# Splitting the third gate/up product's activation sum by token half and moving the small sums around it

## The chip, the cores and the metric

The kernel runs on one core of one Trainium2 chip. The metric is the device time of one execution in microseconds (us), the median of several runs. All engines of the core run their own queues: TensorE (PE) for matmuls, with its weight loads beside it, VectorE (DVE), ScalarE (ACT), GpSimd (POOL), and SyncE (SP), which only issues DMAs here.

## The reference

One encoder layer on 256 prompt tokens and 1024 sample tokens (1280 in all, in fp32), then a final norm. What matters here is the hand-over from the output projection to the SwiGLU feed-forward network:

```python
x = x + mix @ w_o
h2 = rmsnorm(x, ffn_norm_g)
x = x + (jax.nn.silu(h2 @ w_gate) * (h2 @ w_up)) @ w_down
```

`h2` has 1024 columns, `w_gate` and `w_up` are 1024 by 2816.

## The kernel before

**Arithmetic.** Every fp32 operand of a large matmul is split into a high part (a rounding cast, on ACT) and a low part (operand minus high part, on DVE or POOL). One logical product is three matmuls (lines 110 to 112, `mm3`): weight high by moving high, weight high by moving low, weight low by moving high. `h2 @ w_gate` and `h2 @ w_up` are done as block products with seven instead of eight products (a Strassen form): the 1280 tokens are two halves T of 640, the 1024 inner columns two halves K, and the weight is blocks 11, 12, 21, 22. `SEQ` gives the products' order: 1, 2, 6, 7, 4, 5, 3. Each needs one sum of weight blocks and one sum of activation blocks.

**Stages around the change.** In the output projection (loop over ten 128-token tiles t, `NT` = 10) `ffn_in(t, x)` makes each tile of `h2`, transposed, into R["11"] (in the trace zA), R["12"] (zA), R["21"] (zB), R["22"] (zB). For the second half of the tokens (t = 5 to 9) it also makes the activation sums in place: R11 = R12 - R11, then T2[t-5] = R22 - R11, which is product 6's activation sum, then (`differences`) R12 = R22 - R12 and R21 = R21 - T2. For t up to 8 these run on POOL (line 888), for the last tile on DVE. T2[0], T2[1] and T2[4] lie in the buffers named A21, A22 and A12, T2[2] and T2[3] in the two buffers named `sum`.

**Splitting an activation sum.** `split_S` (lines 902 and 903) casts on ACT and subtracts on DVE into the pair S[m], high and low, all 640 columns in one tile each. `build_S(6, ())` does it for the first four 128-column parts of product 6, `split_after` for the fifth; the other products' sums are split in two halves of 320 columns.

**Weights.** `split_A` (lines 909 and 910) casts a weight block on ACT and subtracts on POOL into two of six `wc` buffers. `operand(A, m)` makes the sum first (`sum_A`, line 920, on POOL) where the product has one: for 6, s1 = A21 + A22 into a `sum` buffer, s2 = s1 - A11, the split of s2, and s4 = A12 - s2 for product 3; for 7, A21 = A11 - A21.

**The first round (fp = 0).** Its weight blocks for gate (i = 0) and up (i = 1) are loaded by SP into places `at[0]` to `at[7]` inside the two tiles S5, which are free until product 5. The products are issued as gate 1, gate 2, up 1, up 2, then 6, 7, 4, 5, 3 for gate and up in turn; each has two halves s of 320 tokens with 12 matmuls each. The two halves of a product run in two PSUM banks, products 1 and 2 share them, so product 2 may start only when ACT has copied out product 1 (line 990). Up's copies are held behind the cast of gate's operand 6 (`hold`). In the trace S<-A, S<-sum at lines 902 and 903 are product 6's parts, wc<-S at lines 909 and 910 are splits of weights that lie in the S5 tiles, z<-M at line 990 are product 1's and 2's copies.

**What sets the order.** A planner lays out each engine's queue when the kernel is built, by its own estimate of times, with earlier program text first where several instructions are ready; every engine then runs its queue in order. `tc.issue_after(ins)` queues what is traced in it behind `ins` on the engine of `ins`, and nothing more. SP's queue is in program order. A new tile waits for the users of the earlier tiles on its own bytes; a buffer of a ring waits for the readers of its earlier content.

Of the kernel before, what the change touches and what calls it, by code (L numbers as in the profile page):

```python
# [11 lines left out]
F32 = mybir.dt.float32  # L12
F32R = mybir.dt.float32r
# [26 lines left out]
def encoder_trunk(ctx: ExitStack, tc: tile.TileContext, x_tm, x_T, g_attn, w_c, w_v, w_qk,  # L40
# [46 lines left out]
    def rstd_of(out, ss, n):  # L87
        w = out.shape[1]
        nc.gpsimd.tensor_scalar(out=out, in0=ss, scalar1=1.0 / n, scalar2=EPS,
                                op0=ALU.mult, op1=ALU.add)  # L90
        nc.gpsimd.tensor_tensor(out=out, in0=out, in1=mhalf[:, 0:w], op=ALU.pow)
# [709 lines left out]
    mixed = [None]  # L801
# [48 lines left out]
    def ffn_in(t, x):  # L850
# [3 lines left out]
        nc.scalar.activation(h2, x, AF.Square, accum_out=ss)  # L854
        store(xm_d[t], x)
        rstd_of(r, ss, D)
# [26 lines left out]
        difference(eng, T2[t - 5], R["22"][:, :, cs], R["11"][:, :, cs])  # L883
# [22 lines left out]
    def split_A(raw):  # L906
        hi = rY.tile([P, 4, P], F32R, name="wc", bufs=6)
        lo = rY.tile([P, 4, P], F32R, name="wc", bufs=6)
# [13 lines left out]
    def operand(A, m, s2=None, s4=None):  # L922
        if m == 6:
# [5 lines left out]
            if s4:  # L929
                A["s4"] = rY.tile([P, 4, P], F32, name=s4)  # L930
            else:
                A["s4"] = A["s2"]
            sum_A(A["s4"], A["12"], A["s2"])
# [41 lines left out]
    l4 = [pool("l4a"), pool("l4z"), pool("l4b")]  # L975
    def product(C, w, m, s, held, bank=None, hold=None):
# [5 lines left out]
        for kc in range(4):  # L982
            mm3(ps, w[0][:, kc], w[1][:, kc], S[m][0][:, kc, cs], S[m][1][:, kc, cs],
                kc == 0 and m not in CHAIN, kc == 3, m in CHAIN)
# [38 lines left out]
    def build_S(m, after):  # L1023
        pl, nm = {6: (l4[0], "S6"), 3: (rA, "zA")}.get(m, (l4[2], f"S{m}"))
        S[m] = [pl.tile([P, 4, NQ], F32R, name=nm, bufs=2) for x in "hl"]
        cuts = [(slice(n * P, (n + 1) * P), T2[n]) for n in range(5)] if m == 6 else [
            (slice(s * NS, (s + 1) * NS), None) for s in range(2)]
        for cs, from_ in cuts[:-1] if m == 6 else cuts:
            after = split_after(m, cs, from_, after)
        return after  # L1030

    def split_after(m, cs, from_, after):
        with ExitStack() as es:
            for ins in after:
                es.enter_context(tc.issue_after(ins))
            return split_S(m, cs, from_)
# [26 lines left out]
    s6 = build_S(6, ())  # L1063
    with tc.issue_after(s6[1]):
        cs8 = slice(3 * P, 4 * P)
        difference(nc.vector, R["21"][:, :, cs8], R["21"][:, :, cs8], T2[3])
    for fp in range(NF // 2):
# [3 lines left out]
        if fp == 0:  # L1071
            spare = [l4[2].tile([P, 4, NQ], F32R, name="S5", bufs=2).bitcast(F32)
                     .rearrange("p a b -> p (a b)").rearrange("p (n a b) -> p n a b", n=5, b=P)
                     for _ in range(2)]
            at = [spare[n // 5][:, n % 5] for n in range(8)]
# [18 lines left out]
            with tc.issue_after(w6[0][3]):  # L1094
                w6.append(operand(A0[1], 6, at[7], "A22"))
# [302 lines left out]
```

## Time and profile before

| what | us |
|---|---|
| three runs | 1618.12, 1614.91, 1615.25 |
| median | 1615.25 |
| profiled execution, own time | 1615.65 |
| profiled execution, first to last instruction | 1613.9 |
| PE busy (share of the span) | 1580.4 (98%) |
| POOL busy | 668.8 (41%) |
| DVE busy | 890.7 (55%) |
| ACT busy | 716.0 (44%) |

The gate/up stage lies between 794.5 and about 1346 us of the span; its first round ends near 848.6 us. A share of busy time is a mean over all stages, so what a change in one place is worth is read from the waits and the order of instructions in that place.

### The profile page before, as it was taken

To read this page: it belongs to the slowest core of one execution; us is meant where nothing else is said; L and a number is where in the kernel's file an instruction comes from. 1 tells how busy PE (TensorE), PEld (TensorE's weight loads), DVE (VectorE), ACT (ScalarE), POOL (GpSimd) and SP (SyncE) were. 2 spreads that over 40 slices of the span, in tenths; PEclk is the share of its full clock that TensorE was granted. 3 is DMA by queue.
4 is the path that set the end of the run, shared out by engine and by line. 5 is a ranking of instruction groups with operands and counts; after the bars stand their busy time and mean duration, and the time that the engine had idled before them with its cause. 6 is when DMAs were issued, how large, how long until landed. Compare 5 with 4: busy or idle time off the path is not lost.

```text
span 1613.9 us, 25762 instructions
## 1 busy us (share of the span) xinstructions
PE 1580.4 (98%) x9616; PEld 1442.6 (89%) x9616; DVE 890.7 (55%) x1483; ACT 716.0 (44%) x1484; POOL 668.8 (41%) x839
## 2 busy tenths in 40 slices
PE   8999999999999999999999999999999999999998
PEld 8987899988888888888899999999999998888886
DVE  5743055556677677443493444334444246886676
ACT  6523154555677777544353223232222332443334
POOL 4631444543211119224676665565666651010002
PEclk9999999999999999999999999999999999999999
DMA  8626212152101030234312232222232237843534
GB/s 292 195 78 159 49 26 61 37 201 67 32 16 30 23 119 11 89 118 144 119 63 72 91 110 97 68 90 89 97 110 76 69 128 265 300 139 96 156 103 156
DMA packets 123247, 171.12 MB, mean 106 GB/s; under 512 B 35505, under 2 KB 67505, under 8 KB 123121
## 3 DMA queue, kind: packets, MB, share of 16 engines
q1 hardware_dynamic: 78880, 120.30, 24.3%
q10 hardware_dynamic: 43680, 46.87, 8.4%
q0 software_dynamic: 560, 2.29, 0.3%
q8 instruction: 76, 1.25, 0.3%
q14 instruction: 51, 0.41, 0.1%
HBM read 118.96 MB, written 50.46 MB: 105 GB/s over the span
## 4 chain that ended last, share of the span: by engine, by line
PE 88%; ACT 3%; DVE 3%; POOL 2%; DMA 1%; issue 1%; SPq 0%; ACTq 0%; POOLq 0%; DVEq 0%
PE M L110 10%; PE M L112 10%; PE M L111 10%; PE d L110 5%; PE d L111 5%; PE d L112 5%; PE o L728 4%; PE tp L718 3%; PE na_o L499 2%; PE po L110 2%; PE po L111 2%; PE po L112 2%; PE pj L110 2%; PE pj L112 2%; PE pj L111 2%; PE S L110 2%
## 5 line engine op out<-in xcount | busy, mean ns | idle before, releaser
L110 PE MATMUL M<-S,wc 128*128 128x320 f32 x1056 | 321.9, 309 | 2.8 <-ACT wc L909 1.5
L111 PE MATMUL M<-S,wc 128*128 128x320 f32 x1056 | 324.2, 308 | 0.0
L112 PE MATMUL M<-S,wc 128*128 128x320 f32 x1056 | 312.3, 309 | 0.9 <-POOL wc L910 0.9
L110 PEld LDWEIGHTS M<-S,wc 128*128 128x128 f32 x1056 | 198.0, 188 | 4.0 <-ACT wc L909 2.0
L111 PEld LDWEIGHTS M<-S,wc 128*128 128x128 f32 x1056 | 198.7, 188 | 0.0
L112 PEld LDWEIGHTS M<-S,wc 128*128 128x128 f32 x1056 | 195.2, 188 | 1.2 <-POOL wc L910 1.2
L910 POOL TENSOR_TENSOR wc<-A,wc 128x512 fp32r<-128x512 f32 x86 | 120.7, 1405 | 79.4 <-ACT wc L909 79.3
L992 DVE TENSOR_TENSOR z<-M,z 128x320 f32<-128x320 f32 x120 | 56.4, 487 | 124.0 <-PE M L112 103.5
L910 POOL TENSOR_TENSOR wc<-sum,wc 128x512 fp32r<-128x512 f32 x62 | 88.5, 1427 | 87.0 <-ACT wc L909 86.9
L909 ACT CAST wc<-A 128x512 fp32r<-128x512 f32 x86 | 53.4, 621 | 157.2 <-PE M L111 137.1
L992 DVE TENSOR_TENSOR zB<-M,zB 128x320 f32<-128x320 f32 x100 | 47.6, 488 | 133.4 <-PE M L112 120.1
L111 PE MATMUL d<-S,S 128*128 128x512 f32 (+1 forms) x314 | 121.2, 386 | 0.0
L112 PE MATMUL d<-S,S 128*128 128x512 f32 (+1 forms) x314 | 120.7, 387 | 0.0
L110 PE MATMUL d<-S,S 128*128 128x512 f32 (+1 forms) x314 | 120.5, 387 | 0.0
L100 DVE TENSOR_TENSOR PT<-tp,PT 128x512 fp32r<-128x512 f32 (+1 forms) x144 | 93.0, 658 | 38.9 <-ACT PT L99 37.7
L909 ACT CAST wc<-sum 128x512 fp32r<-128x512 f32 x62 | 38.3, 618 | 145.0 <-PE M L111 93.4
L99 ACT CAST PT<-tp 128x512 fp32r<-128x512 f32 (+1 forms) x144 | 79.4, 566 | 38.2 <-PE tp L718 34.6
L710 DVE TENSOR_REDUCE mm<-S 128x1 f32<-128x1024 f32 (+1 forms) x80 | 84.8, 1062 | 10.9 <-PE S L112 9.4
L1039 ACT CAST S<-as 128x640 fp32r<-128x640 f32 x58 | 42.2, 728 | 105.5 <-issue 60.2
L741 POOL TENSOR_TENSOR ob<-ob 128x128 f32<-128x128 f32 x40 | 18.4, 461 | 157.2 <-ACT ob L738 149.2
L712 ACT ACTIVATE ex<-S,mm 128x1024 f32<-128x1024 f32 (+1 forms) x80 | 79.7, 996 | 8.0 <-DVE mm L710 7.4
L728 PE MATMUL o<-PT,v 128*128 128x256 f32 x544 | 80.6, 287 | 1.0 <-ACT PT L99 1.0
(429 smaller groups left out, 4120.8 us busy)
## 6 DMA issues: line engine op xcount, KB each, us to landing
as<-act_d SPq DMA_DIRECT2D x73, 320.0 KB
w<-in_w_down_dram SPq DMA_DIRECT2D x44, 256.0 KB
act_d<-z ACTq DMA_DIRECT2D x35, 320.0 KB
act_d<-zB ACTq DMA_DIRECT2D x35, 320.0 KB
A<-in_w_gate_dram SPq DMA_DIRECT2D x42, 256.0 KB
A<-in_w_up_dram SPq DMA_DIRECT2D x42, 256.0 KB
x<-in_x_tm_dram SPq DMA_DIRECT2D x20, 512.0 KB
cT_d<-stg ACTq DMA_DIRECT2D x20, 320.0 KB
```

The source lines that it names most:

```text
L99: i = nc.scalar.copy(out=hi, in_=ps)
L100: nc.vector.tensor_sub(out=lo, in0=ps, in1=hi)
L110: nc.tensor.matmul(out, lhsT=sh, rhs=mh, start=first, stop=False, **kw)
L111: nc.tensor.matmul(out, lhsT=sh, rhs=ml, start=False, stop=False, **kw)
L112: return nc.tensor.matmul(out, lhsT=sl, rhs=mh, start=False, stop=last, **kw).ins
L710: nc.vector.reduce_max(out=nm[:, u:u + 1], in_=S, axis=AX.X, negate=True)
L712: nc.scalar.activation(ex, S, AF.Exp, bias=nm[:, u:u + 1], scale=1.0, accum_out=l[:, u:u + 1])
L718: nc.tensor.transpose(tp[:, j], ex[:, kt * P:(kt + 1) * P], ident)
L728: nc.tensor.matmul(oT, lhsT=vv, rhs=pt[s][g][:, j], start=kt == 0 and s == 0, stop=kt == nkt - 1 and s == 1)
L909: i0 = nc.scalar.copy(out=hi, in_=raw)
L910: i1 = nc.gpsimd.tensor_tensor(out=lo, in0=raw, in1=hi, op=ALU.subtract)
L992: nc.vector.tensor_add(out=o, in0=ps, in1=a)
```

## The change

- **Product 6's activation sum** is kept in four tiles: high and low, for each token half s. `part6(n)` splits 128-column part n into them; part 2 lies across the two halves and is split in two pieces. Part 2 is split first, parts 0 and 1 are queued on ACT behind the last tile's squaring (`last_sq`, line 854), part 3 and part 4 come inside the fp = 0 loop. `product` picks the half's tile for m = 6.
- **T2[3]** (t = 8) is not made in `ffn_in` but on POOL behind the low part of gate's operand 6; part 3 and R21 - T2[3] follow it.
- **Up's operand 2** is split before the loop, its low part on DVE instead of POOL, into places inside the second S5 tile instead of `wc` buffers.
- **Later sums on POOL**: operand 7 is queued behind the low part of up's operand 6; the two s4 (`sum_4`, for product 3) behind the low part of up's operand 7. Before, all of them could be queued as soon as they were ready.
- **Places**: the pool l4b, which held S5, S7 and S4, becomes three: l4b (S5), l4c (one tile S4), l4d (the other S4, and S7). `at[0]` to `at[4]` stay in the first S5 tile, `at[5]` and `at[7]` are in the S4 tile of l4d, `at[6]` in that of l4c, so S4 is written only when s4 of gate and of up have read them.
- `build_S(7)` is queued behind the cast of up's operand 6 on ACT alone. `rstd_of` returns its instruction, `last_rs` isn't used.

```diff
-        nc.scalar.activation(h2, x, AF.Square, accum_out=ss)
+        last_sq[0] = nc.scalar.activation(h2, x, AF.Square, accum_out=ss).ins
...
-        difference(eng, T2[t - 5], R["22"][:, :, cs], R["11"][:, :, cs])
+        if t != NT - 2:
+            difference(eng, T2[t - 5], R["22"][:, :, cs], R["11"][:, :, cs])
...
+    def sum_4(A, nm=None):
+        A["s4"] = rY.tile([P, 4, P], F32, name=nm) if nm else A["s2"]
+        sum_A(A["s4"], A["12"], A["s2"])
...
-            sum_A(A["s4"], A["12"], A["s2"])
+            if s2 is None:
+                sum_4(A)
...
-    l4 = [pool("l4a"), pool("l4z"), pool("l4b")]
+    l4 = [pool("l4a"), pool("l4z"), pool("l4b"), pool("l4c"), pool("l4d")]
...
+            sh, sl = [x[s][:, kc] if m == 6 else x[:, kc, cs] for x in S[m]]
+            mm3(ps, w[0][:, kc], w[1][:, kc], sh, sl, kc == 0 and m not in CHAIN, kc == 3, m in CHAIN)
...
+    def part6(n, after=()):
+        with ExitStack() as es:
+            for ins in after:
+                es.enter_context(tc.issue_after(ins))
+            for s in range(2):
+                a, b = max(n * P, s * NS), min((n + 1) * P, (s + 1) * NS)
+                if a < b:
+                    src = T2[n][:, :, a - n * P:b - n * P]
+                    hi, lo = [x[s][:, :, a - s * NS:b - s * NS] for x in S[6]]
+                    i0 = nc.scalar.copy(out=hi, in_=src).ins
+                    i1 = nc.vector.tensor_sub(out=lo, in0=src, in1=hi).ins
+        return i0, i1
...
-    s6 = build_S(6, ())
-    with tc.issue_after(s6[1]):
-        cs8 = slice(3 * P, 4 * P)
-        difference(nc.vector, R["21"][:, :, cs8], R["21"][:, :, cs8], T2[3])
+    at = blocks(l4[2], "S5", F32)
+    w0[2, 1] = hi, lo = blocks(l4[2], "S5", F32R)[0:2]
+    nc.scalar.copy(out=hi, in_=A0[1]["12"])
+    nc.vector.tensor_sub(out=lo, in0=A0[1]["12"], in1=hi)
+    b, c = blocks(l4[4], "S4", F32, 1), blocks(l4[3], "S4", F32, 1)
+    at += [b[0], c[0], b[1]]
+    S[6] = [[l4[0].tile([P, 4, NS], F32R, name="S6", bufs=4) for _ in range(2)] for _ in range(2)]
+    cs8 = slice(3 * P, 4 * P)
+    part6(2)
+    for n in range(2):
+        part6(n, (last_sq[0],))
...
-                    w0[2, 1] = operand(A0[1], 2)
                     A0[1]["12"] = load_A(1, 0, "12", at[5])
-                    w6 = [operand(A0[0], 6, at[6], "A21")]
+                    w6 = [operand(A0[0], 6, at[6])]
                     hold = w6[0][2]
-                    s6 = split_after(6, slice(4 * P, 5 * P), T2[4], (hold, s6[1]))
+                    with tc.issue_after(w6[0][3]):
+                        difference(nc.gpsimd, T2[3], R["22"][:, :, cs8], R["11"][:, :, cs8])
+                    s6 = part6(3)
+                    with tc.issue_after(s6[1]):
+                        difference(nc.vector, R["21"][:, :, cs8], R["21"][:, :, cs8], T2[3])
+                    s6 = part6(4, s6)
...
-                w = w6 if m == 6 else [operand(A0[i], m) for i in range(2)]
+                with ExitStack() as es:
+                    if m == 7:
+                        es.enter_context(tc.issue_after(w6[1][3]))
+                    w = w6 if m == 6 else [operand(A0[i], m) for i in range(2)]
+                if m == 7:
+                    with tc.issue_after(w[1][3]):
+                        for i in range(2):
+                            sum_4(A0[i], ("A21", "A22")[i])
                 if m != 3:
-                    build_S(SEQ[n + 3], w[1][2:])
+                    build_S(SEQ[n + 3], w[1][2:3] if m == 6 else w[1][2:])
```

## Rows read from the trace of the kernel before

**Rows 1.** The page's busy times: us (share of the span) and number of instructions of an engine.

```profile
PE 1580.4 (98%) x9616; PEld 1442.6 (89%) x9616; DVE 890.7 (55%) x1483; ACT 716.0 (44%) x1484; POOL 668.8 (41%) x839
```

**Rows 2.** The waits of PE over the whole span, those of the gate/up products: who waited for whom, us in total, times, longest us.

```profile
PE M L110 <- ACT wc L909: 1.5, 2, 0.9
PE M L110 <- ACT S L902: 1.2, 1, 1.2
...
PE M L112 <- POOL wc L910: 0.9, 1, 0.9
```

**Rows 3.** PE in order of time, 805 to 815 us and at 853 us: start, us, what, and in brackets the idle time before it with what ended it.

```profile
805.61 0.46 PE L112 MATMUL M<-S,wc 128*128 128x320 f32 x2
806.95 0.41 PE L110 MATMUL M<-S,wc 128*128 128x320 f32 x1 [0.89 <-ACT wc L909]
...
808.75 0.96 PE L110 MATMUL M<-S,wc 128*128 128x320 f32 x2 [1.24 <-ACT S L902]
809.50 0.47 PE L111 MATMUL M<-S,wc 128*128 128x320 f32 x1
...
811.63 0.33 PE L110 MATMUL M<-S,wc 128*128 128x320 f32 x1
...
813.56 0.31 PE L111 MATMUL M<-S,wc 128*128 128x320 f32 x1
...
813.86 0.31 PE L111 MATMUL M<-S,wc 128*128 128x320 f32 x1
...
814.15 0.31 PE L110 MATMUL M<-S,wc 128*128 128x320 f32 x1
...
853.80 0.42 PE L112 MATMUL M<-S,wc 128*128 128x320 f32 x1 [0.93 <-POOL wc L910]
```

**Rows 4.** Busy time by stretch: the first row counts only instructions that write or read the products' PSUM tile M (columns: stretch, length, then PE, PEld, DVE, ACT busy with counts, granted PE clock as a share of full speed, DMA share, GB/s), the others all instructions (with a column for POOL after ACT's).

```profile
794.47:806.07 11.60, 10.96 (x72) 10.46 (x71) 0.00 (x0) 1.45 (x4) 1.00 0.56 183
...
794.47:806.07 11.60, 11.59 (x81) 11.32 (x79) 10.39 (x9) 6.73 (x19) 10.96 (x9) 1.00 0.56 183
806.07:813.86 7.79, 5.67 (x28) 5.38 (x29) 6.91 (x6) 3.66 (x8) 7.71 (x5) 0.78 0.13 34
...
809.00:810.00 1.00, 1.00 (x4) 0.96 (x5) 1.00 (x2) 0.35 (x2) 1.00 (x2) 0.50 0.00 0
...
848.60:860.00 11.40, 10.47 (x72) 10.21 (x71) 6.11 (x6) 3.65 (x8) 8.17 (x6) 1.00 0.38 132
```

**Rows 5.** ACT in order of time, 795 to 809 us.

```profile
795.22 0.64 ACT L902 CAST S<-A 128x512 fp32r<-128x512 f32 x1
...
796.77 1.08 ACT L854 ACTIVATE m<-x 128x1024 f32<-128x1024 f32 x1
...
805.95 0.43 ACT L990 COPY z<-M 128x320 f32<-128x320 f32 x1 [0.89 <-PE M L112]
806.28 0.62 ACT L909 CAST wc<-S 128x512 fp32r<-128x512 f32 x1
808.08 0.62 ACT L902 CAST S<-A 128x512 fp32r<-128x512 f32 x1 [1.18 <-DVE A L888]
808.60 0.75 ACT L990 COPY z<-M 128x320 f32<-128x320 f32 x2
```

**Rows 6.** POOL in order of time, 795 to 825 us, and one instruction of the second round.

```profile
795.91 1.84 POOL L888 TENSOR_TENSOR sum<-zB,zA 128x512 f32<-128x512 f32 x1
...
799.37 1.30 POOL L910 TENSOR_TENSOR wc<-A,wc 128x512 fp32r<-128x512 f32 x1
800.63 1.75 POOL L920 TENSOR_TENSOR sum<-S 128x512 f32<-128x512 f32 x1
802.46 1.65 POOL L920 TENSOR_TENSOR S<-sum,A 128x512 f32<-128x512 f32 x1
804.05 1.76 POOL L920 TENSOR_TENSOR S<-A,S 128x512 f32<-128x512 f32 x1
...
807.46 1.72 POOL L910 TENSOR_TENSOR wc<-S,wc 128x512 fp32r<-128x512 f32 x1
...
815.96 8.82 POOL L910 TENSOR_TENSOR wc<-S,wc 128x512 fp32r<-128x512 f32 x4
...
860.27 1.30 POOL L910 TENSOR_TENSOR wc<-A,wc 128x512 fp32r<-128x512 f32 x1 [3.43 <-ACT wc L909]
```

**Rows 7.** DVE in order of time, 798 to 824 us.

```profile
798.22 0.68 DVE L903 TENSOR_TENSOR S<-sum,S 128x512 fp32r<-128x512 f32 x1
...
801.14 1.79 DVE L903 TENSOR_TENSOR S<-sum,S 128x512 fp32r<-128x512 f32 x1
802.85 1.79 DVE L888 TENSOR_TENSOR zB<-zB,sum 128x512 f32<-128x512 f32 x1
804.57 0.68 DVE L869 TENSOR_TENSOR zA<-trh,gf 128x512 f32<-128x512 f32 x1
...
816.07 2.54 DVE L903 TENSOR_TENSOR S<-zA,S 128x1280 fp32r<-128x1280 f32 x1
...
821.45 2.18 DVE L903 TENSOR_TENSOR S<-zB,S 128x1280 fp32r<-128x1280 f32 x1
```

**Rows 8.** SP's DMA queue in order of time, the last of the six weight loads into the S5 tiles and what follows it.

```profile
795.62 1.19 SPq L64 DMA_DIRECT2D S<-in_w_up_dram  x1
805.84 35.56 SPq L64 DMA_DIRECT2D A<-in_w_gate_dram  x4
```

More of the change, by code (lines that the diff above doesn't have):

```diff
@@ L90, in rstd_of @@
                                 op0=ALU.mult, op1=ALU.add)
-        nc.gpsimd.tensor_tensor(out=out, in0=out, in1=mhalf[:, 0:w], op=ALU.pow)
+        return nc.gpsimd.tensor_tensor(out=out, in0=out, in1=mhalf[:, 0:w], op=ALU.pow).ins
     def split_w(hi, lo, raw):
@@ L799, in load_wo @@
             wo.append(wt)
-    mixed = [None]
+    mixed, last_sq, last_rs = [None], [None], [None]
     def mix_in(t):
@@ L906, in split_A @@
     def split_A(raw):
-        hi = rY.tile([P, 4, P], F32R, name="wc", bufs=6)
-        lo = rY.tile([P, 4, P], F32R, name="wc", bufs=6)
+        hi, lo = [rY.tile([P, 4, P], F32R, name="wc", bufs=6) for _ in range(2)]
         i0 = nc.scalar.copy(out=hi, in_=raw)
@@ L920, in sum_A, with operand @@
         nc.gpsimd.tensor_tensor(out=out, in0=a, in1=b, op=op)
-    def operand(A, m, s2=None, s4=None):
+    def sum_4(A, nm=None):
+        A["s4"] = rY.tile([P, 4, P], F32, name=nm) if nm else A["s2"]
+        sum_A(A["s4"], A["12"], A["s2"])
+    def operand(A, m, s2=None):
         if m == 6:
@@ L928, in operand @@
             w = split_A(A["s2"])
[L929 to L932, printed above, removed]
-            sum_A(A["s4"], A["12"], A["s2"])
+            if s2 is None:
+                sum_4(A)
             return w
@@ L1023, in build_S, with split_after @@
     def build_S(m, after):
[L1024 to L1029, printed above, removed]
+        pl = {3: [rA] * 2, 5: [l4[2]] * 2, 7: [l4[4]] * 2, 4: l4[3:5]}[m]
+        S[m] = [x.tile([P, 4, NQ], F32R, name="zA" if m == 3 else f"S{m}", bufs=1 if m == 4 else 2)
+                for x in pl]
+        for s in range(2):
+            after = split_after(m, slice(s * NS, (s + 1) * NS), after)
         return after
-    def split_after(m, cs, from_, after):
+    def split_after(m, cs, after):
         with ExitStack() as es:
@@ L1035, in split_after @@
                 es.enter_context(tc.issue_after(ins))
-            return split_S(m, cs, from_)
+            return split_S(m, cs)
+    def part6(n, after=()):
+        with ExitStack() as es:
+            for ins in after:
+                es.enter_context(tc.issue_after(ins))
+            for s in range(2):
+                a, b = max(n * P, s * NS), min((n + 1) * P, (s + 1) * NS)
[5 more added lines that the diff above has]
+        return i0, i1
     def split_f(o, raw):
@@ L1061, in down_first, with blocks @@
             ops[5, f] = a_ring[f], w_ring[f]
-    s6 = build_S(6, ())
-    with tc.issue_after(s6[1]):
-        cs8 = slice(3 * P, 4 * P)
-        difference(nc.vector, R["21"][:, :, cs8], R["21"][:, :, cs8], T2[3])
+    def blocks(pl, nm, dt, bufs=2):
+        x = pl.tile([P, 4, NQ], F32R, name=nm, bufs=bufs)
+        x = (x.bitcast(F32) if dt is F32 else x).rearrange("p a b -> p (a b)")
+        x = x.rearrange("p (n a b) -> p n a b", n=5, b=P)
+        return [x[:, n] for n in range(5)]
+    at = blocks(l4[2], "S5", F32)
[9 more added lines that the diff above has]
+        part6(n, (last_sq[0],))
     for fp in range(NF // 2):
@@ L1071, in encoder_trunk @@
         if fp == 0:
[L1072 to L1075, printed above, removed]
             for n, (b, i) in enumerate((("21", 0), ("22", 0), ("21", 1), ("22", 1), ("12", 0),
```

6 lines of the change are left out of this document (2 added, 4 removed).

## The prediction

> **What bounds the kernel now.** I read the page's busy times first: PE is busy for 98% of the span [rows 1], so only the few places where PE stands idle can give anything, unless matmuls are saved, and the change saves none. The waits of PE show what belongs to the gate/up products: three causes, 3.3 us in all [rows 2]; two of the entries have their longest wait in the stretch below. PE in order of time then shows the place that the change touches [rows 3]. From 794.47 to 806.07 us 72 matmuls of 320 columns ran [rows 4], three products of 24: gate 1, up 1, gate 2. The next two waits are 0.89 us for a cast of ACT and 1.24 us for another [rows 3]. ACT's rows name them: wc<-S, the cast of gate's operand 6 (806.28 to 806.90), and S<-A, the last part of product 6's activation sum (808.08 to 808.70) [rows 5]. So the planner had put three matmuls of product 6 ahead of up's product 2, and PE, which runs its queue in order, waited for both. Up 2 could not have filled the place either: the copies of up 1, held behind the first cast, stand behind the second too, at 808.60 [rows 5]. After this idle time the granted clock was 0.50 of full speed, the level of 1.2 GHz [rows 4], and matmuls were (811.63 - 809.50) / 8 = 0.266 us apart instead of (814.15 - 813.56) / 4 = 0.147 [rows 3].
>
> **What the place costs.** From 806.07 to 813.86 PE did the 24 matmuls of up 2 and three of product 6: 27 x 0.147 = 3.97 us of work in 7.79. The loss is 3.82 us: 2.13 idle, about 12 x 0.119 = 1.4 from the clock, the rest between. This is the most that the change can win here. The other wait, 0.93 us at 853.80 [rows 3], lies in the second round, after loads that wait for PE's progress in the first; I leave it where it is, with 0.9 either way in the range. It also shows that an idle time of 0.93 alone left the clock at 1.00 [rows 4].
>
> **The change, part by part.** *Squaring earlier.* ACT cast three parts of product 6 from 795.22 on before the squaring at 796.77 [rows 5]. Parts 0 and 1 now follow it; up's operand 2 and part 2's two pieces may still precede it. Bounds: 0 to 1.4 us earlier; I take 0.7, the middle, since what may still precede it is about half of the three casts. *Operand 2's low part* leaves POOL: 1.30 us [rows 6], and costs DVE one subtract, 0.68 alone to 1.79 beside POOL [rows 7], at a time when DVE only waits for the last tile's scale. With both, POOL starts s1 of gate's operand 6 at 800.63 - 1.3 - 0.7 = 798.6. *T2[3]* leaves POOL's queue ahead of that scale: 1.84 us [rows 6] that ended before the squaring did, so nothing there, and comes back later (below). *Part 2 in two pieces* adds one cast and one subtract; both run before the scale is ready: nothing if so, 0.4 + 0.7 us on ACT and DVE if not. *Four tiles* let product 6's first half start without parts 3 and 4. *Loads*: SP's order is unchanged. The last load's new place covers bytes of the old stage's small gain vector, which DVE's scaling of the last tile reads until 804.57 + 0.68 = 805.25 [rows 7]; SP's next issue came at 805.84 [rows 8], so only this load waits, from 795.62, and its reader, s4 of up, comes after 820. Nothing, and none of the following loads moves.
>
> So gate's operand 6: s1, s2, cast, low part. A POOL instruction of this size took 1.30 us alone and 1.65 to 1.76 beside DVE [rows 6]; I take 1.6, as POOL is sometimes alone in the new order. s2 ends at 798.6 + 3.2 = 801.8, the cast (0.62 + 0.1 for the hand-over) at 802.5, the low part at 804.1. The cast thus falls ahead of ACT's copy at 805.95, up 1's copies follow, and up 2 can start at 806.07. The place closes; product 6 of gate starts at 806.07 + 24 x 0.147 = 809.6 instead of 813.7.
>
> **What is late next.** Now PE wants everything 3.8 us earlier, and POOL, which was busy for 7.71 of the 7.79 us [rows 4], gets two new holds and one chain. The chain: T2[3] on POOL 804.1 to 805.7; ACT's cast 806.4; part 3's low part 0.7 (POOL waits, so DVE is alone) 807.2; R21 - T2[3] 0.7, 807.9. Only then is the second `sum` buffer free for s1 of up's operand 6: 809.5, s2 811.1, cast 811.8, low part 813.4. PE needs this at up 6's third matmul: 809.6 + 24 x 0.147 + 0.3 = 813.4. Just in time. Queued behind it, by the new hold, are operand 7's sums (before: S<-A,S already at 804.05 [rows 6]): 815.0 and 816.6, then gate 7's low part at 818.2. PE needs it at 809.6 + 48 x 0.147 + 0.3 = 816.95: **1.25 us late**. In all, ten POOL instructions from 798.6 on and 3.6 us of waits for ACT and DVE: 798.6 + 3.6 + 10 x 1.6 = 818.2. After that PE is 1.25 behind and the rest fits: up 7's low part 819.8 for 821.7; s4 twice, 823.0; S4's tile is then free for DVE's first half, 2.18 [rows 7], at 825.2 for 825.1; product 4's low parts 824.6 and 826.2 for 825.4 and 828.9. On DVE, product 7's first half ended at 818.61 [rows 7] and is wanted at 816.8; DVE stood idle for 11.60 - 10.39 and 7.79 - 6.91, 2.1 us before it [rows 4], which must serve; up to 0.5 us late.
>
> **Sum.** 3.82 - 1.25 = 2.6 us won. The profiled execution took 1615.65, with 1.75 outside its span, 0.4 above the median; taken off the median, 1615.25 - 2.6 = 1612.7. With DVE's possible 0.5 I say **1612.8**.
>
> A price that decides is that of a POOL instruction beside DVE. A pair of subtracts, 0.68 on DVE and 1.30 on POOL alone, would take 1.98 if one fully waited for the other; POOL's starts beside a busy DVE lie 1.6 to 1.8 apart [rows 6], so part of each overlaps. The Trainium skill, page "SBUF — State Buffer", section "Who interferes with whom", says that a DVE instruction with two SBUF inputs contends with a GpSimd instruction that reads SBUF and that the second "fully blocks" until the first finishes: by that rule the ten would take 1.98 each where DVE always has a subtract ready; the rows stand a little below it. That is rival D.
>
> **Rivals.**
> - **B, the whole gain stays**: the holds leave POOL alone for most of the chain, at 1.30 us: 798.6 + 3.6 + 13.0 = 815.2, before 816.95; or the planner lets PE do the matmuls with high weights of product 7 first, eight in a half, which for 8 x 0.147 = 1.2 us need no low part. For it: POOL waits for DVE and ACT three times in the chain, and the planner already put matmuls out of order at 806.95. 1615.25 - 3.8 = 1611.4, or to 1610.6 with part of the 0.93.
> - **C, no change**: the planner again puts matmuls of product 6 ahead of up 2 and they wait, or gate's cast stays behind ACT's copy at 805.95 and 1.3 us remain there, on top of product 7's 1.25 and some clock. Then 3.82 - 1.3 - 1.25 - about 0.9 = 0.4: 1614.9. This includes that the early cast, the change's purpose, doesn't come about.
> - **D, slower**: each of the ten POOL instructions waits out one DVE subtract. Place: the chain through the second `sum` buffer and operand 7's hold. 798.6 + 3.6 + 10 x 1.98 = 822.0, 5.05 us late at gate 7; an idle time of that length would bring the lower clock again, 1.4 by the rows at 809: 1615.25 - 3.82 + 5.05 + 1.4 = 1617.9. It eats the gain from a mean of about 1.8 us on (818.2 + 2.0 to 2.6). For it: four POOL instructions beside DVE's subtracts of 1280 elements took 8.82 us, 2.2 each [rows 6, 7]. Against: three of the ten find DVE waiting.
>
> **How the numbers follow.** Forecast A (1612.0 to 1614.0) 0.40, B 0.27, C (1614.0 to 1616.5) 0.19, D (1616.5 to 1620.5) 0.14. 0.2% is 3.2 us, about what a measurement of this kernel can tell from no change. Faster by more than that, below 1612.0: B and the edge of A, 0.32. Slower, above 1618.5: the part of D in which the clock falls a second time at product 4, 0.09. Within: 0.59. The range takes in A, C, most of B and the lowest of D: 1610.8 to 1617.0.
>
> **What would show it.** Right: no wait of PE between 806 and 809.6, PE's clock at 1.00 there, gate's cast of operand 6 before 804 on ACT; POOL's s1 for up starting only behind R21 - T2[3] on DVE, and a wait of about 1 us of PE for POOL at product 7. B: no such wait. C: a wait for ACT at 806 again. D: POOL's instructions 2 us apart from 804 to 822, a wait over 3 us at product 7 and the clock at 0.50 behind it. The prediction is wrong in its ground if PE waits before 806, or if the second round shifts by more than the first did.

## The result, and the profile after

The changed kernel took 1621.17 us (median of 22 runs, 1617.27 to 1624.28) beside 1617.74 (22 runs, 1614.49 to 1620.18) for the kernel before: a ratio of 1.0018, 95% interval 1.0011 to 1.0024 (it is not the quotient of the two medians, which is 1.0021). By the ratio it is slower by about 2.9 us, where 2.4 less was forecast and the top of the range was 1617.0. The forecast started from the 1615.25 of three runs; carried over to 1617.74, its range would end at 1619.5, which is still below 1621.17. The profiled execution took 1622.45, with a span of 1620.3. In experiments 5, 8 and 11 one execution each took over 4000 us; the ratios leave it out, and the medians in their table would move by at most 0.15 us without it.

The two traces are compared from the stage's first product matmul on (M1), which starts at 794.47 before [rows 4] and at 800.37 after: up to there PE runs the same instructions in both, and that part differs between executions (the eleventh experiment, which has before's program up to there, had M1 at 797.92; more under Open). The end of the comparison is a copy of ACT late in gate's second round, which in every kernel here waits about 1.49 us for the same work of PE. ACT in order of time, before and then after:

```profile
880.49 0.43 ACT L990 COPY zB<-M 128x320 f32<-128x320 f32 x1 [1.49 <-PE M L112]
```

```profile
888.25 0.43 ACT L991 COPY zB<-M 128x320 f32<-128x320 f32 x1 [1.49 <-PE M L112]
```

M1 to this copy is 86.02 us before and 87.88 after: **1.86 us are lost here**, inside the 1.8 to 3.9 that the interval gives. I call this stretch the section below.

After's page and waits of PE over the whole span (us in total, times, longest), beside [rows 1, 2]:

```profile
PE 1583.5 (98%) x9616; PEld 1444.7 (89%) x9616; DVE 887.6 (55%) x1485; ACT 716.6 (44%) x1485; POOL 663.4 (41%) x838
```

```profile
PE M L112 <- POOL wc L910: 2.7, 2, 2.1
PE M L110 <- ACT wc L909: 1.2, 1, 1.2
PE M L111 <- DVE S L904: 0.5, 1, 0.5
```

PE of after in order of time, beside [rows 3]:

```profile
800.37 0.30 PE L110 MATMUL M<-S,wc 128*128 128x320 f32 x1
...
809.92 0.63 PE L866 MATMUL trh<-ident,m 128*128 128x128 f32 x4 [0.60 <-DVE m L857]
...
812.59 0.31 PE L110 MATMUL M<-S,S 128*128 128x320 f32 x1
...
816.10 0.31 PE L110 MATMUL M<-S,wc 128*128 128x320 f32 x1
...
816.54 0.31 PE L110 MATMUL M<-S,wc 128*128 128x320 f32 x1
...
825.19 0.42 PE L110 MATMUL M<-S,wc 128*128 128x320 f32 x1 [1.24 <-ACT wc L909]
827.02 0.41 PE L112 MATMUL M<-S,wc 128*128 128x320 f32 x1 [0.58 <-POOL wc L910]
...
835.88 0.42 PE L111 MATMUL M<-S,wc 128*128 128x320 f32 x1 [0.47 <-DVE S L904]
...
861.56 0.42 PE L112 MATMUL M<-S,wc 128*128 128x320 f32 x1 [2.10 <-POOL wc L910]
```

Read it in three parts. *The place of before is closed*: up 2 (its weights are in S tiles now, M<-S,S) runs from 812.59 and product 6 from 816.10 with no wait; only the last tile's transposes were waited for, 0.60. Before, three matmuls of product 6 and all of up 2 were done at 813.86, 19.39 us after M1; after, the fourth matmul of product 6 starts at 816.54, 16.17 after M1. Gain 3.22. *Products 7 and 4 have waits*, 1.24, 0.58 and 0.47, that before had not. *The second round's wait* is 2.10 in place of 0.93.

Busy time by stretch (columns as in the second kind of [rows 4]): the second row is up 2, the third runs from product 6 to the end of product 5, the fourth into the second round.

```profile
800.37:811.96 11.59, 10.99 (x77) 10.76 (x76) 6.48 (x9) 6.32 (x17) 6.60 (x7) 1.00 0.48 161
811.96:816.10 4.14, 4.14 (x30) 4.14 (x29) 3.31 (x5) 2.93 (x8) 2.02 (x2) 1.00 0.19 52
816.10:848.20 32.10, 29.73 (x195) 28.24 (x194) 28.38 (x27) 17.77 (x21) 24.87 (x15) 1.00 0.12 37
848.20:863.66 15.46, 13.36 (x91) 13.10 (x91) 13.63 (x15) 4.50 (x8) 12.31 (x9) 1.00 0.42 155
```

The third row has 32.10 - 29.73 = 2.4 us in which PE stands, and 195 x 0.147 = 28.7 for what it does, so another 1.0 in matmuls further apart around the waits. The clock is 1.00 in all four.

SP's queue and POOL of after in order of time, beside [rows 8, 6]:

```profile
800.56 1.31 SPq L64 DMA_DIRECT2D S<-in_w_gate_dram  x2
...
814.25 0.33 SPq L64 DMA_DIRECT2D S<-in_w_up_dram  x1
822.00 1.31 SPq L64 DMA_DIRECT2D A<-in_w_gate_dram  x2
```

```profile
806.14 1.29 POOL L920 TENSOR_TENSOR sum<-S 128x512 f32<-128x512 f32 x1 [2.75 <-DMA S<-in_w_gate_dram]
807.39 0.56 POOL L91 TENSOR_TENSOR rh<-rh,mhalf 128x1 f32<-128x1 f32 x1
807.91 1.31 POOL L920 TENSOR_TENSOR S<-sum,A 128x512 f32<-128x512 f32 x1
809.96 1.28 POOL L910 TENSOR_TENSOR wc<-S,wc 128x512 fp32r<-128x512 f32 x1 [0.73 <-ACT wc L909]
811.19 1.30 POOL L889 TENSOR_TENSOR sum<-zB,zA 128x512 f32<-128x512 f32 x1
814.61 1.62 POOL L920 TENSOR_TENSOR sum<-S 128x512 f32<-128x512 f32 x1 [2.12 <-ACT z L991]
816.31 1.64 POOL L920 TENSOR_TENSOR S<-sum,A 128x512 f32<-128x512 f32 x1
818.68 1.58 POOL L910 TENSOR_TENSOR wc<-S,wc 128x512 fp32r<-128x512 f32 x1 [0.73 <-ACT wc L909]
820.21 4.27 POOL L920 TENSOR_TENSOR S<-A,S 128x512 f32<-128x512 f32 x2
824.45 2.52 POOL L910 TENSOR_TENSOR wc<-S,wc 128x512 fp32r<-128x512 f32 x1
...
856.58 1.30 POOL L920 TENSOR_TENSOR A<-A,A 128x512 f32<-128x512 f32 x1
...
859.66 1.84 POOL L910 TENSOR_TENSOR wc<-sum,wc 128x512 fp32r<-128x512 f32 x1
```

The first three lines of POOL are what the prediction lacked: s1 of gate's operand 6 waits 2.75 us for its weight loads, which SP issued only at 800.56, and the last tile's scale (L91, 807.39) stands behind s1 in POOL's queue. From there the ten instructions run to 826.97, and PE takes the last one's result at 827.02. The last two lines, the sum for gate's operand 7 and the low part of operand 6, lie ahead of the second round's wait.

SP's waits by whom they end, 780 to 830 us, in the kernel before and then after, tell why the loads were late:

```profile
SPq L64 <- PE po L112: 16.9, 1, 16.9
```

```profile
SPq L64 <- PE po L112: 18.4, 1, 18.4
```

Both wait for the output projection (po). After, the issue at 800.56 follows the last po matmul, which starts at 800.14; before, the loads went out at 793.09, 1.38 us *ahead* of M1, with po matmuls still to come. The po matmul that starts 0.42 us ahead of the first issue, before and then after:

```profile
792.67 0.40 PE L112 MATMUL po<-wo,mT 128*128 128x512 f32 x1
```

```profile
800.14 0.39 PE L112 MATMUL po<-wo,mT 128*128 128x512 f32 x1
```

It is the last one on the seventh of the eight `wo` weight tiles before, and on the eighth after. The first S5 tile, in which the loads land, got another place in memory: the new split of up's operand 2 took the place that the raw weights had before, and their new one lies over weights that the last po matmuls read. In the built programs the tile of the raw weights lies at bytes 58528 to 68768 of each partition before, over the third, fourth and seventh `wo` tile, and at 68768 to 79008 after, over the seventh and eighth.

### The profile page after: what moved, and what is told of

Its sections match the earlier page's. It is cut to its first block, busy times and chain, and to the rows that moved or that the text cites. A ratio compares the mean times of both kernels' runs of the same rounds, so it can differ in the third digit from the quotient of the medians.

```text
span 1620.3 us, 25768 instructions
## 1 busy us (share of the span) xinstructions
PE 1583.5 (98%) x9616; PEld 1444.7 (89%) x9616; DVE 887.6 (55%) x1485; ACT 716.6 (44%) x1485; POOL 663.4 (41%) x838
## 3 DMA queue, kind: packets, MB, share of 16 engines
q8 instruction: 76, 1.25, 0.3%
## 4 chain that ended last, share of the span: by engine, by line
PE 89%; POOL 3%; ACT 2%; DVE 2%; issue 2%; DMA 1%; ACTq 0%; SPq 0%; POOLq 0%; DVEq 0%
PE M L112 10%; PE M L111 10%; PE M L110 10%; PE d L110 5%; PE d L111 5%; PE d L112 5%; PE o L728 4%; PE tp L718 3%; PE na_o L499 3%; PE po L110 2%; PE po L111 2%; PE po L112 2%; PE pj L110 2%; PE pj L112 2%; PE pj L111 2%; PE S L110 2%
## 5 line engine op out<-in xcount | busy, mean ns | idle before, releaser
L111 PEld LDWEIGHTS M<-S,wc 128*128 128x128 f32 x1048 | 196.6, 188 | 1.4 <-DVE S L904 1.3
L110 PEld LDWEIGHTS M<-S,wc 128*128 128x128 f32 x1048 | 195.9, 188 | 1.8 <-ACT wc L909 1.5
L112 PEld LDWEIGHTS M<-S,wc 128*128 128x128 f32 x1048 | 193.2, 188 | 3.4 <-POOL wc L910 3.4
```

The costliest lines, as they stand in the source:

```text
L110: nc.tensor.matmul(out, lhsT=sh, rhs=mh, start=first, stop=False, **kw)
L111: nc.tensor.matmul(out, lhsT=sh, rhs=ml, start=False, stop=False, **kw)
L112: return nc.tensor.matmul(out, lhsT=sl, rhs=mh, start=False, stop=last, **kw).ins
```

## Experiments

All build on the changed kernel unless said otherwise; each ran in five rounds beside the kernel before. "Section" is M1 to the copy of ACT, from one trace; before has 86.02. Where the clock fell to 1.2 GHz in a trace, that is part of its section: in before, 8 and 11 at the place of before, in 1, 3 and 5 in the second round, in 2 and 4 at product 7, and in the others nowhere. A section is one trace and a ratio 6 to 22 runs; they differ by up to 2 us (in 6, -1.79 beside a ratio of 1.0000). A section says where that trace's time went, the ratio what a version costs.

| | kernel | ratio to before (95%) | median, us | section, us | against before |
|---|---|---|---|---|---|
| | after | 1.0018 (1.0011 to 1.0024) | 1621.17 | 87.88 | +1.86 |
| 1 | scale first | 1.0015 (1.0003 to 1.0027) | 1620.99 | 89.41 | +3.39 |
| 2 | loads at the old bytes | 1.0003 (0.9992 to 1.0013) | 1618.56 | 86.39 | +0.37 |
| 3 | 1 and 2 | 1.0004 (0.9994 to 1.0013) | 1618.78 | 87.54 | +1.52 |
| 4 | no holds | 1.0033 (1.0021 to 1.0046) | 1624.62 | 90.82 | +4.80 |
| 5 | 3 and T2[3] early | 1.0001 (0.9992 to 1.0011) | 1616.87 | 87.51 | +1.49 |
| 6 | 3 and second round's order | 1.0000 (0.9991 to 1.0008) | 1616.77 | 84.23 | -1.79 |
| 7 | 5 and 6 | 0.9987 (0.9977 to 0.9998) | 1614.85 | 84.16 | -1.86 |
| 8 | before, low part on DVE | 1.0009 (0.9999 to 1.0020) | 1618.77 | 87.90 | +1.88 |
| 9 | 7, gate's sum for 7 unheld | 0.9984 (0.9973 to 0.9996) | 1614.34 | 83.79 | -2.23 |
| 10 | 9, s4 earlier | 0.9996 (0.9983 to 1.0008) | 1616.85 | 83.94 | -2.08 |
| 11 | before, second round's order | 0.9999 (0.9988 to 1.0009) | 1617.26 | 85.20 | -0.82 |
| 12 | 9 with T2[3] and scale as in the change | 0.9988 (0.9976 to 1.0000) | 1615.41 | 84.24 | -1.78 |

**1. The scale ahead of s1.**

```diff
-                    w6 = [operand(A0[0], 6, at[6])]
+                    with tc.issue_after(last_rs[0]):
+                        w6 = [operand(A0[0], 6, at[6])]
```

> The changed kernel, with gate's operand 6 queued on GpSimd behind the last tile's scale (both its instructions). In the changed kernel the second of them, L91, stood behind the sum s1, which waited 2.75 us for a weight load. Theory A (the late weight loads set GpSimd's whole chain, s1 at 5.8 us after the stage's first product matmul): the scale comes 3 us earlier, PE's wait of 0.60 us for the transposes goes, but s1 still starts at 5.8 and the waits of PE at product 7 (1.24 and 0.58) stay: 0 to 1 us faster than the changed kernel, so a ratio to before of 1.0012 to 1.0018. Rival B (the late scale, through the last tile's T2, part 4 and DVE's subtracts, sets product 7): the waits at product 7 go too, 2 to 3 us faster, ratio 1.0000 to 1.0005. Rival C (the two holds on GpSimd set it): as A.

The transposes no longer wait, and POOL's chain stays late: s1 waits 3.00 us for the loads (804.70, 6.67 after M1). The ratio is that of the change; the section is 1.5 longer, but here the clock fell behind the second round's wait, some 1.4 us at the price of [rows 3]. So the late scale, which I took for a second cause, costs nothing that can be measured here.

**2. The loads at the bytes they had before.** The raw tile and the split of up's operand 2 change places.

```diff
-    at = blocks(l4[2], "S5", F32)
-    w0[2, 1] = hi, lo = blocks(l4[2], "S5", F32R)[0:2]
+    at = blocks(l4[2], "S5", F32, 1)
+    w0[2, 1] = hi, lo = blocks(l4[2], "S5x", F32R, 1)[0:2]
```

> The changed kernel, with the first five raw weights in the lower of the two S5 places again, as before, and up's operand 2 in the upper one (names of their own instead of a ring of two). Theory A: the first load is issued 1.5 us ahead of the stage instead of 0.2 behind, s1 starts at about 4.2 instead of 5.8 us, and all that follows on GpSimd comes 1.6 us earlier: the waits at product 7 shrink from 1.8 to at most 0.5 and the losses from there to product 3 from 3.7 to about 2; 1.5 to 2.5 us faster than the changed kernel, ratio 1.0003 to 1.0009. Rival B (late scale): s1 and with it L91 come 1.6 us earlier too, so the same sign but without change at product 7 if e1 has none. Rival C (holds): less than 0.7 us faster, ratio 1.0014 to 1.0018, since the holds keep the order.

The first load in SP's queue, and then POOL:

```profile
796.62 0.80 SPq L64 DMA_DIRECT2D S<-in_w_gate_dram  x2
```

```profile
801.68 1.44 POOL L920 TENSOR_TENSOR sum<-S 128x512 f32<-128x512 f32 x1 [0.66 <-DMA S<-in_w_gate_dram]
```

With M1 at 798.00 the loads start at -1.38 again, as before, and s1 at 3.68 in place of 5.77. The ratio falls from 1.0018 to 1.0003 (the two intervals overlap by 0.0002), the section by 1.5. **The place of the raw weights is most of what was lost against the kernel before.** The expected gain is not there yet. PE at the start of product 6 and where it takes the chain's last result:

```profile
812.95 0.31 PE L110 MATMUL M<-S,wc 128*128 128x320 f32 x1
...
823.20 0.41 PE L112 MATMUL M<-S,wc 128*128 128x320 f32 x1 [0.57 <-POOL wc L910]
```

Product 6 starts 14.95 after M1, where 15.1 was forecast: by its fourth matmul 4.0 us are won. But the ten POOL instructions take 21.5 us from s1 to this result, where the forecast has 19.6. PE waits 0.78 and 0.57 at product 7, about the forecast's 1.25 in all, and the clock falls behind it, some 1.4 us; the second round's wait is 1.63 for 0.93. This takes back 3.5 of the 4.4 us that the section shows; 0.9 I can't place.

**3. Both.**

> Both edits together: the scale ahead of gate's operand 6, and the raw weights in the lower S5 place. Theory A: s1 starts behind the scale or its load, at 4.2 to 4.6 us, the transposes come at 8 as before, and PE goes without waits to product 6; 2.5 to 3.5 us faster than the changed kernel, ratio 0.9997 to 1.0003. Rival C (holds): 1 us at most, ratio 1.0012 or more, with the waits at product 7 unchanged.

No better than 2 in time. POOL stands idle 2.68 us (it was 2.12) before s1 of *up's* operand 6, which starts 12.82 after M1 beside 12.76 in the second experiment, although gate's low part starts 0.54 earlier: T2[3], part 3 and R21 - T2[3] set it, and on DVE the last tile's sum T2[4] (808.90) now stands ahead of part 3's low part. In the second round PE then ran at the lower clock (granted clock is the third column from the right):

```profile
856.00:858.00 2.00, 0.57 (x4) 0.57 (x5) 1.97 (x2) 0.62 (x1) 1.92 (x2) 1.00 0.42 164
858.00:860.00 2.00, 2.00 (x10) 2.00 (x10) 0.05 (x1) 0.43 (x1) 2.00 (x2) 0.60 0.43 162
860.00:862.00 2.00, 2.00 (x9) 2.00 (x9) 0.00 (x0) 0.00 (x0) 0.43 (x1) 0.55 0.67 157
```

Some 12 matmuls 0.267 apart in place of 0.147 are 1.4 us of the section of 87.54.

**4. No holds.** Operand 7's sums and both s4 run as soon as they are ready, as before the change.

```diff
-                        es.enter_context(tc.issue_after(w6[1][3]))
...
-                    with tc.issue_after(w[1][3]):
-                        for i in range(2):
-                            sum_4(A0[i], ("A21", "A22")[i])
...
+                    sum_4(A0[0], "A21")
...
+                sum_4(A0[1], "A22")
```

> The changed kernel without its two holds on GpSimd: operand 7's sums and s4 may be queued as soon as they are ready, as in the kernel before; late loads and late scale stay. Rival C (the holds set product 7 and, through S4's places, product 4): PE's waits there fall from 2.3 us to under 1, 1.5 to 3 us faster than the changed kernel, ratio 1.0000 to 1.0009. Theory A (late start): GpSimd does the same instructions in the same time from the same late start, so what is won at product 7 is lost at product 6: within 0.7 us of the changed kernel, ratio 1.0014 to 1.0022.

Slower by 0.15% than the change (six runs; the two intervals overlap by 0.0003). PE waits at products 6 and 7:

```profile
818.22 0.41 PE L110 MATMUL M<-S,wc 128*128 128x320 f32 x1 [1.61 <-ACT wc L909]
...
821.06 0.42 PE L110 MATMUL M<-S,wc 128*128 128x320 f32 x1 [1.99 <-ACT wc L909]
822.29 0.64 PE L111 MATMUL M<-S,wc 128*128 128x320 f32 x1 [0.81 <-DVE S L904]
```

The holds are worth having: without them gate's sum for 7 and s4 stand ahead of the low part of gate's operand 6 on POOL, and everything of up's comes later. Behind these waits the clock was 0.50 from 822 to 828, which is part of the 4.80. Rival C of this run falls.

**5. T2[3] in `ffn_in` again** (on 3).

```diff
-        if t != NT - 2:
-            difference(eng, T2[t - 5], R["22"][:, :, cs], R["11"][:, :, cs])
+        difference(eng, T2[t - 5], R["22"][:, :, cs], R["11"][:, :, cs])
...
-                    with tc.issue_after(w6[0][3]):
-                        difference(nc.gpsimd, T2[3], R["22"][:, :, cs8], R["11"][:, :, cs8])
```

> The third experiment's kernel (late tile's scale ahead of gate's operand 6, weight loads at the lower bytes) with T2[3] made in ffn_in again, as before the change. In the third experiment POOL stands idle 2.68 us (810.93, for DVE's R21 - T2[3]) before s1 of up's operand 6, and PE then waits 1.58 us for a cast of operand 7 (822.28). Theory (the chain through the second sum buffer, T2[3] to part 3 to R21 to s1, makes operand 7 late): s1 of up starts at about 9.5 us after the stage's first product matmul in place of 12.8, PE's wait at product 7 is gone, and as the second round's loads follow PE's progress, the time falls by 1.0 to 1.6 us: 1617.2 to 1617.8 beside 1618.8. Rival (PE is held at the second round in any case, so what is won at product 7 is waited for there): the wait at product 7 goes, that at the second round's product 6 grows from 2.10 to about 3.5, time 1618.8. Second rival: T2[3] on POOL ahead of the scale delays the scale and s1 by 0.4, and transposes come late: 1619.2.

The section stays (87.51), also with the lower clock in the second round; s1 of up starts at 12.24, not at 9.5. POOL of the seventh experiment, which has the same order here, shows why:

```profile
804.25 1.68 POOL L919 TENSOR_TENSOR sum<-S 128x512 f32<-128x512 f32 x1 [1.80 <-DVE S L1049]
```

Now s1 of *gate's* operand 6 waits 1.80 us for DVE's subtract of part 2, which reads T2[2] in the other `sum` buffer. The chain through the two buffers was moved from up to gate, not removed. My theory for this run fell.

**6. The change's hold, used in the second round** (on 3).

```diff
-                    w = operand(A, m)
+                    with ExitStack() as es:
+                        if m == 7 and fp == 1 and i == 0:
+                            es.enter_context(tc.issue_after(lo6))
+                        w = operand(A, m)
+                    if m == 6:
+                        lo6 = w[3]
```

> The third experiment's kernel with the change's own hold used once more, in the second round: the sum of gate's operand 7 is queued on POOL behind the low part of operand 6 (fp = 1, i = 0). In the third experiment PE waits 2.10 us there (857.43) for that low part, and POOL's sum for operand 7 (852.44, 1.30) and a low part of operand 2 lie ahead of it. Theory (POOL's order in the second round sets that wait): the wait falls by 1.3, to about 0.8, time 1617.5 beside 1618.8. Rival (the wait is set by the loads, which land when PE's first round lets them): POOL's earlier place is empty time, the wait stays at 2.1, time 1618.8. Second rival: operand 7 of that round comes late instead, PE waits as long 3.5 us later: 1618.8 with another wait.

PE's wait there:

```profile
853.64 0.42 PE L112 MATMUL M<-S,wc 128*128 128x320 f32 x1 [0.33 <-POOL wc L910]
```

2.10 has become 0.33, and the clock stayed at 1.00; the section falls by 3.3 (1.8 of wait, 1.4 of clock). The ratios, 1.0004 and 1.0000, can't be told apart; the medians, 2.0 apart, were taken on different chips. POOL's order, not the loads, sets the second round's wait: its loads begin 21.0 us after M1 (817.11), as late as in the change (21.6).

**7. Both of these.**

> Both edits of the two kernels before at once. If both places count and don't cover each other: 1618.8 - 1.3 - 1.3 = 1616.2, some 0.0007 below the kernel before. If the second round takes back what product 7 gives: 1617.5. If neither counts: 1618.8.

0.9987: the first version whose interval lies below before. By the section (84.16 beside 84.23 in 6) nothing of this comes from T2[3]'s place, and the interval overlaps that of 6.

**8. One part of the change alone, on the kernel before.**

```diff
-                    w0[2, 1] = operand(A0[1], 2)
+                    w0[2, 1] = hi, lo = [rY.tile([P, 4, P], F32R, name="wc", bufs=6)
+                                         for _ in range(2)]
+                    nc.scalar.copy(out=hi, in_=A0[1]["12"])
+                    nc.vector.tensor_sub(out=lo, in0=A0[1]["12"], in1=hi)
```

> The kernel before with one part of the change alone: up's operand 2 keeps its place in the program and its wc buffers, but its low part is a subtract of DVE instead of POOL. POOL starts s1 of gate's operand 6 some 1.3 us earlier (4.9 us after the stage's first product matmul in place of 6.2). Theory (the idle time at 806 comes from the order that the planner gave ACT and PE, not from POOL's pace): the cast of operand 6 stays behind ACT's copies, so PE's two waits there stay, POOL's later chain gains 1.3 that nothing asks for: same time as before, 1617.4, within 0.5. Rival (POOL's pace sets the place): PE's waits of 0.89 and 1.24 shrink by 1.3 and the time falls by 1.3 to 2.0: 1615.4 to 1616.1.

POOL's s1 moved up as expected (4.81 after M1), and ACT's and PE's order stayed; but the section grew by 1.88. DVE, and then PE:

```profile
805.38 1.78 DVE L1085 TENSOR_TENSOR wc<-A,wc 128x512 fp32r<-128x512 f32 x1
807.09 0.68 DVE L869 TENSOR_TENSOR zA<-trh,gf 128x512 f32<-128x512 f32 x1
```

```profile
810.86 0.96 PE L110 MATMUL M<-S,wc 128*128 128x320 f32 x2 [2.44 <-ACT S L902]
```

The subtract stands ahead of the last tile's scaling on DVE, 1.78 us long, and part 4 of product 6 comes that much later: 2.44 of wait for 1.24 [rows 3]; the clock, too, was lower for longer (0.50 from 810 to 816). The ratio, 1.0009 (0.9999 to 1.0020), can't tell this from nothing. Of the two places tried, the low part does well on DVE in the change's, before the loop, where DVE waits for the scale.

**9. Gate's sum for 7 unheld** (on 7).

```diff
-                with ExitStack() as es:
-                    if m == 7:
-                        es.enter_context(tc.issue_after(w6[1][3]))
-                    w = w6 if m == 6 else [operand(A0[i], m) for i in range(2)]
+                w = list(w6) if m == 6 else []
+                for i in range(2 - len(w)):
+                    with ExitStack() as es:
+                        if m == 7 and i == 1:
+                            es.enter_context(tc.issue_after(w6[1][3]))
+                        w.append(operand(A0[i], m))
```

> The seventh experiment's kernel with the change's hold of operand 7 kept for up alone: gate's A11 - A21 may run on POOL as soon as it is ready, and comes to stand between s2 and the low part of gate's operand 6, where POOL stood idle 0.79 us for ACT's cast. In the seventh experiment PE waits 1.13 us (821.60) for the cast of gate's operand 7, whose sum was queued behind the low part of up's operand 6, and 1.14 us (831.56) for DVE at product 4. Theory (the hold makes gate's operand 7 late, its sum being one of ten POOL instructions in a row): the low part of gate's operand 6 moves 0.9 later, to 13.2 us after the stage's first product matmul where 15.2 is wanted, the cast of gate's operand 7 follows at once, the wait of 1.13 goes; up's low part ends near 18.9 for 18.8. Time lower by about 1.1, at most 2.2 if DVE's wait goes as well: 0.0007 to 0.0014 below the seventh. Rival (what is missing is POOL's time, not its order): up's operand 6 or 7 comes 0.9 late instead, and the time stays.

PE's waits of the gate/up products over the whole span:

```profile
PE M L112 <- POOL wc L909: 0.9, 1, 0.9
PE M L110 <- DVE z L992: 0.9, 2, 0.5
```

The cast's wait is gone; of it 0.92 comes back at the low part of gate's operand 7, and DVE's wait falls from 1.14 to 0.43 and 0.49. The section is 0.4 shorter, not 1.1: some of each theory. At 0.9984 (0.9973 to 0.9996) this is **the lowest ratio of all, about 2.6 us below the kernel before**; it can't be told from 7 and 12, whose intervals overlap it.

**10. s4 behind gate's low part of 7** (on 9): `issue_after(w[0][3])` in place of `w[1][3]`.

> The kernel of the ninth experiment with the two s4 queued on POOL behind the low part of gate's operand 7 instead of up's. In the seventh experiment ACT waits 2.59 us (824.66) for s4 of up before it may write product 4's first half, since the weights that s4 reads lie in the S4 tile; DVE's subtract then runs 826.01 to 831.0, and DVE's addition for product 4's bank comes behind it: PE waits 1.14. Theory (the new places tie S4 to s4): s4 of up ends 1.3 to 1.6 earlier, the cast and DVE's subtract follow, the wait of 1.14 goes: another 1.1 below the ninth. Rival (up's low part of operand 7, now behind the two s4, comes late): PE waits 0.3 to 1.0 for POOL at up 7, time as the ninth or 1 above.

The 0.92 stays, up's low part of 7 is waited for (0.26), and DVE's 1.14 at product 4 is back, though S4's first subtract starts earlier: the additions for PSUM queue behind both of its subtracts. The rival holds in the waits; the section is 0.15 longer than the ninth's and the ratio 0.0012 higher, with intervals that overlap.

**11. The sixth edit on the kernel before.**

> The kernel before with the sixth experiment's edit alone: the sum for gate's operand 7 of the second round queued on POOL behind the low part of operand 6. In the kernel before PE waits 0.93 us there, and POOL's sum takes 1.29 just ahead of it. Theory (the wait at the second round is POOL's order, not part of the change): the wait goes, time lower by about 0.9, ratio 0.9994; so of the seventh experiment's gain about half is not the change's. Rival (the loads set it): same time as before, and the gain of the seventh is the change's alone.

The wait of 0.93 is gone in the trace and the section is 0.82 shorter, as the theory has it; the ratio of 0.9999 (0.9988 to 1.0009) can't tell that from nothing. By the sections, 0.8 of the ninth's 2.2 us are not the change's.

**12. The ninth with T2[3] and the scale as the change has them.**

> The second experiment's kernel (weight loads at the lower bytes, T2[3] behind the low part of gate's operand 6 as in the change, no hold for the late tile's scale) with the two edits of POOL's order: gate's A11 - A21 of the first round unheld, that of the second round behind the low part of operand 6. It differs from the ninth in T2[3] and the scale alone. In the second experiment POOL stands idle 2.12 us before s1 of up's operand 6, for DVE's R21 - T2[3]; in the seventh 1.80 before s1 of gate's, for DVE's subtract of part 2, which reads the other sum buffer. Theory (one of the two sum buffers is late either way, so where T2[3] is made changes little): s1 of up at about 13.2 us after the stage's first product matmul as in the ninth, time as the ninth, 0.9980 to 0.9988 of before. Rival (T2[3] on POOL behind the low part is what costs): 0.9995 of before or above.

S1 of up starts at 14.15, 1.0 later than in the ninth, and the section is 0.45 longer; the intervals overlap. Between the two ways to make T2[3] there is little.

## Why the prediction was wrong

**The place at 806: right.** ACT's cast of gate's operand 6 fell ahead of the copies, the planner put up 2 first, the clock stayed at 1.00. 3.22 of 3.82 came, and the missing 0.60 is the wait for the transposes. That wait lies 9.55 after M1, which is 804.0 in the time of the kernel before: the forecast's own sign, a wait ahead of 806, came true. Its cause is the scale behind s1 in POOL's queue (it is gone in the first experiment), and in the second, with the loads on time, it is not there either.

**"Loads: Nothing, and none of the following loads moves": the step that failed first.** I looked at the order of SP's queue, which did stay, and at the bytes of the last load, but not at where the first S5 tile itself would lie. It started the loads 1.57 us later against M1. The chain of ten was to start at 798.6, 4.1 after M1, and started at 5.77. The second experiment shows this cause. The following loads moved as well: the first one for the second round went out at 822.00, 21.6 after M1, for 11.4 before [rows 8]. The hold on gate's sum for 7 did this, since without it, in the ninth experiment, that load goes out 11.5 after M1 again (807.92), for 20.5 in the seventh (818.42). No wait of PE is seen to come of it: in the seventh, with the late load, PE has none in the second round.

**The chain itself: right in order, but too short; the mis-sized term of the sum.** The ten took 1.68 us in the mean, where 1.6 was taken: seven of 1.28 to 1.64, the two sums for 7 at 2.13, the last 2.52. What lay between them (L91's 0.56 with it) was 4.0 for 3.6. Gate 7's low part was wanted at 816.10 + 48 x 0.147 + 0.3 = 823.46 and came at 827.02: 3.56 late, where the prediction had 1.25. Of the difference, 1.67 is the start, 0.8 the durations, 0.4 the idle time, less 0.6 by which PE itself was later. So the chain was some 1.2 too short besides its late start, and in the second experiment, which starts it in time, 1.9 (21.5 for 19.6).

**The second round's wait "left where it is": the second failed step.** The forecast allowed 0.9 either way for it in the range and nothing in the sum. It cost 2.10 - 0.93 = 1.17. After, POOL's s1 of that round stands behind a low part and starts 3.1 us later against M1 than before, while the sum for 7, 1.30, lies ahead of the low part that PE wants. The sixth experiment shows that POOL's order is the cause.

**The sum after the fact.** With 3.22 won, 1.17 lost in the second round and 1.86 lost in all, 3.9 must have gone back between product 6 and there. The stretch shows 3.4 of it, 2.4 idle and 1.0 in slower matmuls; 0.5 I can't place.

**Rivals.** D had the place right (operand 7's hold, behind the chain) and nearly the time, but not the cause: the pace was nearer to A's 1.6 than to 1.98, the result was 3.56 late and not 5.05, and the clock did not fall in the change. That its time comes out is luck. C's fear that the early cast wouldn't come about was unfounded. B's whole gain, 3.8 us, came in no run; experiments 7 and 9 have 2.1 and 2.6, a gain of A's size, once the loads and the second round are mended, and by the eleventh some 0.8 of it is not the change's.

One reading of the forecast was off: the waits in [rows 2] add up to 3.6 us, not 3.3. Nothing else rests on it.

On rival D's rule: one pair shows it at work. POOL's T2[3] ran from 811.19 for 1.30 us, and DVE's subtract beside it, here:

```profile
811.31 1.73 DVE L889 TENSOR_TENSOR zA<-zA 128x512 f32<-128x512 f32 x1
```

It ended at 813.04, 0.55 after POOL's; alone such a one takes 0.69. The Trainium skill, page "SBUF — State Buffer", section "Who interferes with whom", would have it start when POOL ends and so, as an estimate, end at 813.18; the row agrees to 0.14. Here it was DVE that paid. The first four of POOL's ten, this one among them, took 1.28 to 1.31, the price of POOL alone, and the other six 1.58 to 2.52 beside DVE, so that the mean stayed at 1.68.

**Open.** The new places of `at[5]` to `at[7]` in the S4 tiles were not undone by themselves. They hold SP's sixth load to 814.25 in the change (795.62 before, [rows 8]), for which no one waits in the trace, and tie product 4's cast to s4. M1 lay between 796.1 and 800.4 in the changed kernels and between 794.5 and 797.9 in the three that start as before. This difference stands already some 145 us earlier, where no instruction is changed: ACT's first squaring ahead of the output projection (line 813) starts at 647.58 before and at 653.75 after, and from there to M1 it is 146.5 to 147.0 us in every trace. Why executions differ by then stays open; it is a reason to read the section beside the whole time.

## What to carry to other kernels

When a change allocates a new tile in a pool, ask which earlier tile's bytes every tile of that pool now gets, and who last reads them: the queue's order can stay word for word while its first load starts 1.6 us later. When a place is closed, follow the gain through to the next place that is set by an engine's order and not by PE's progress (here POOL's in the second round): a wait that is "not part of this" takes back what comes early. And a hold that orders one engine's queue is cheap to try at every place that has the same chain.

## What was not expected of the hardware

**An idle time's length alone does not tell whether TensorE's clock falls.** PE stood 2.10 us ahead of the second round's product 6 in the change and went on at 1.00; after the same 2.10 in the third experiment, 2.09 in the first and 1.89 in the fifth, the granted clock was 0.50 to 0.66 for some 3 to 4 us, the level of 1.2 GHz. In the second experiment idle times of 0.78 and 0.57 at product 7 were followed by 0.50:

```profile
822.00:824.00 2.00, 1.43 (x7) 1.10 (x7) 0.81 (x3) 0.00 (x0) 2.00 (x2) 0.89 0.00 0
824.00:826.00 2.00, 2.00 (x9) 2.00 (x8) 0.00 (x1) 0.36 (x1) 2.00 (x3) 0.50 0.00 0
826.00:828.00 2.00, 2.00 (x12) 2.00 (x12) 1.51 (x2) 2.00 (x3) 2.00 (x2) 0.76 0.00 0
```

while 1.13 and 1.14 in the seventh left it at 1.00. With some 1.4 us at stake each time, a trace's section can be that much off a kernel's usual one, which is why it is read here beside the ratio.
